# A two-layer decoder trunk on one core: down projections with 34 seven-product quads whose weight sums are made in DRAM by accumulating DMAs

## The chip, the core and the metric

The kernel runs on one core of one Trainium2 chip. A core has a matrix engine (TensorE, "PE" in the profile; its weight loads are "PEld"), a vector engine (VectorE, "DVE"), a scalar engine (ScalarE, "ACT"), GpSimd ("POOL") and SyncE ("SP"); the last two do little here but issue DMAs. Each engine runs its own instructions in order, and waits for others through semaphores. Sixteen DMA engines move the data between DRAM and the core's memory. The metric is the device time of one execution in microseconds.

## The reference

The input is 256 tokens by 2048 features in float32. Two layers follow one another, each with attention (block attention in the first, sliding window with sinks in the second) and a gated feed-forward with a causal convolution of width 3. Each half of a layer ends with a residual and a layer norm. The change lies in the feed-forward:

```python
def conv_ffn(x, w_up, conv_w, conv_b, w_down):
    h = x @ w_up                                    # 2048 -> 2 x 5504
    ...                                             # causal depthwise convolution, width 3
    g, v = jnp.split(hc, 2, axis=-1)
    return (jax.nn.gelu(g) * v) @ w_down            # 5504 -> 2048
...
h = layer_norm(ALPHA * h + ffn, ln_g[layer, 1], ln_b[layer, 1])
```

## The kernel before

All products are made in float32r from split operands: a number is held as a high part and the rest, and a product takes three matmuls (high by high, high by low, low by high). The weights come through one stream. A *half* is 128 x 1024 weights, 512 KB. `load_weights` (L98) puts the next half into one of four raw buffers by a DMA of SP's queue; `high_upto` (L113) lets ScalarE write its high part (L129), `low_piece` (L156) lets VectorE write the rest (L158). When a half is split its raw buffer is free, and the next load is issued. `take` (L202) hands the next half to TensorE and splits three halves ahead, or as far as `reach` says.

The work runs in stages: attention, output projection, up projection with convolution and gate, down projection, twice. The order on each engine is the order of the program text. A *step* is one half of weights that TensorE has used; `at(n, f)` puts the call `f` n steps further on in the program text. It sets no time by itself: an engine reaches the instruction when those before it on the same engine are done and its semaphores allow it.

In the output projection of the attention (32 halves) the dictionary `reach`, filled by `settle` (L403), makes the splits run up to 14 halves ahead of TensorE, into places of `xT`, `up` and `st` that are free then. Near its end the first 128 tokens are finished before the second 128 (`tilewise`, L345, and `late`, L583): VectorE folds in the accumulators (L435), takes the moments and norms the first tokens (L564, L565) while TensorE works on the second; TensorE then transposes the normed tokens (`turn`, L570, matmuls at L574) between its products. The last splits that `reach` asks for stand ahead of these steps on VectorE and ScalarE.

When the attention's memory is given back, `FeedForward.__call__` (L810) lets POOL load the convolution's weights `cw` (L817), and in layer 0 four copies from DRAM to DRAM, `band<-ud` (L286).

The up projection has 86 units of two halves (`ws_unit`, L296). After each unit comes a convolution on VectorE, and after each pair of units the gate and the split of the result into `st` or `up`.

The down projection (`project_out` with `paired`, and `two_chunks`, L478) works on two chunks of 512 columns at a time, 43 blocks of 128 rows each. Some blocks form *quads*: two row blocks by two column chunks, for two tiles of 128 tokens. A quad is a 2 x 2 matrix product with seven products in place of eight, on sums of the activations and sums of the weights; three sums of products go to PSUM banks of their own (`a`, `s1`, `s2`, `s3`) and are combined after the last quad. Before, there are six quads in each pair of chunks, 24 in all. VectorE makes their sums of weights from the raw halves (`quad_high`, L140, and `quad_low`, L151; the subtractions are at L137), and the sums of activations at the start of the down projection (`sums`, L443). The plain products of the other blocks lie between the quads.

```python
    for i, n in enumerate(groups):
        order += [plain.pop(0) for _ in range(n - 1)] + [(2 * i, 0)]
        quads.append(len(order) // 2)
        order += [(2 * i, 1), (2 * i + 1, 1), (2 * i + 1, 0), plain.pop(0)]
```

Of the kernel before, what the change touches and what calls it, by code (L numbers as in the profile page):

```python
# [53 lines left out]
class Quad(namedtuple("Quad", "tm uh ul bh bl")):  # L54
# [3 lines left out]
    def third(self, i):  # L58
        return self.tm[:, i * 512:(i + 1) * 512]

    def shape(self, b):
        return b.rearrange("p (a c) -> p a c", c=P)


def paired_order(lead, groups):

    plain = [(k, c) for c in range(2) for k in range(2 * PAIRS, FT)]
    order, quads = [plain.pop(0) for _ in range(lead)], []  # L70
    for i, n in enumerate(groups):
        order += [plain.pop(0) for _ in range(n - 1)] + [(2 * i, 0)]
        quads.append(len(order) // 2)
        order += [(2 * i, 1), (2 * i + 1, 1), (2 * i + 1, 0), plain.pop(0)]
    return order + plain, quads
# [3 lines left out]
def trunk(ctx: ExitStack, tc: tile.TileContext, wst, xT_in, x_in, relb, onehot, umask, sinks, conv_in, ln_g, ln_b, out):  # L79
# [11 lines left out]
    n_halves = wst.shape[0]  # L91
    raws, halves, aside, quad = {}, {}, {}, {}
# [20 lines left out]
    def high_upto(i, behind=None):  # L113
        while todo["high"] <= min(i, n_halves - 1):
# [20 lines left out]

    def minus(out, a, b):
        nc.vector.tensor_tensor(out=out, in0=a, in1=b, op=ALU.subtract)  # L137

    def quad_high(s):


        q, (wh, wl) = quad[s], placed[s]
        b11, b12, b22 = raws[s - 1][:, 512:], raws[s][:, 0:512], raws[s][:, 512:]
        t3, t1, t2 = (q.third(i) for i in range(3))
        nc.scalar.activation(q.bh, q.shape(b22), AF.Copy)
        minus(t1, b12, b11)
        minus(t3, b22, b12)
        nc.scalar.activation(wh, q.tm[:, 0:HW], AF.Copy)  # L148
        minus(t2, b22, t1)

    def quad_low(s):  # L151
        q, (wh, wl) = quad[s], placed[s]
        minus(q.bl, q.shape(raws[s][:, 512:]), q.bh.bitcast(F32))
        minus(wl, q.tm[:, 0:HW], wh.bitcast(F32))
# [5 lines left out]
    def split_upto(i, behind=None):  # L160
        while todo["low"] <= min(i, n_halves - 1):
            s = todo["low"]
            high_upto(s, behind)
            if s in quad:
                quad_low(s)
                raws.pop(s - 1)
                load_weights()
            elif len(pieces(s)) == 1:
                if s - 1 in quad:
                    q = quad[s - 1]  # L170
                    nc.scalar.activation(q.uh, q.tm[:, 512:], AF.Copy)
                low_piece(s, slice(0, HW))
                if s - 1 in quad:
                    minus(q.ul, q.tm[:, 512:], q.uh.bitcast(F32))
            placed.pop(s)
            todo["low"] += 1
            if s + 1 not in quad:
                raws.pop(s)
                load_weights()
# [86 lines left out]
    def bias_table(pool):  # L266
# [15 lines left out]
        pe_at(3, table)  # L282

# [112 lines left out]
    def project_out(src, nk, li, homes, preload, turnover=None, paired=None):  # L396
# [5 lines left out]
        w0 = nexth["i"] + (nk * NCH - WINDOW_BLOCKS) // 2  # L402
# [18 lines left out]
        gb = gbp.tile([P, 2, D], F32, name="gb")  # L421
# [24 lines left out]
        def sums(p, n):  # L446


            a, b = (xT[:, 2 * p + i:2 * (p + n):2, :] for i in range(2))
            f, sm = (gb[:, i, 0:n * 512].rearrange("p (a b) -> p a b", b=512) for i in range(2))  # L450
            x = lambda i, t: f[:, :, i * T + t * P:i * T + (t + 1) * P]
            s = lambda i: sm[:, :, (i - 1) * P:i * P]

            def whole():
                for i in range(2):
                    y = st[:, 2 * p + i:2 * (p + n):2, :].bitcast(F32)
                    nc.vector.tensor_tensor(out=f[:, :, i * T:(i + 1) * T], in0=y[:, :, 0:T], in1=y[:, :, T:2 * T],
                                            op=ALU.add)

            def combine():  # L460
                nc.vector.tensor_tensor(out=s(1), in0=x(1, 1), in1=x(0, 1), op=ALU.add)
                minus(s(2), s(1), x(0, 0))
                minus(s(3), x(0, 0), x(0, 1))
                minus(s(4), x(1, 0), s(2))

            def split():
                nc.scalar.activation(a, sm, AF.Copy)
                minus(b, sm, a.bitcast(F32))

            return whole, combine, split  # L470

        def two_chunks(n):


            order, quads = paired_order(LEAD[n // 2], GROUPS[n // 2])
            i0 = nexth["i"]
            accs = [[acc_tile(), acc_tile()], []]
            side = {}  # L478
            tail = WINDOW_BLOCKS if n else 0
            place = lambda k, t: (src(k)[:, t * P:(t + 1) * P], src(k)[:, T + t * P:T + (t + 1) * P])  # L480
            total = lambda p, i: (xT[:, 2 * p, (i - 1) * P:i * P], xT[:, 2 * p + 1, (i - 1) * P:i * P])
            begun = set()

            def product(key, acc, a, wh, wl, stop=False):
                nc.tensor.matmul(acc, a[0], wh, start=key not in begun, stop=False)  # L485
                nc.tensor.matmul(acc, a[0], wl, start=False, stop=False)  # L486
                nc.tensor.matmul(acc, a[1], wh, start=False, stop=stop)  # L487
                begun.add(key)

            def bank(name):  # L490
                if name not in side:
                    side[name] = psum.tile([P, 512], F32, name="at")
                return side[name]

            def acc(c, t):
                if not accs[c]:
                    accs[c] += [acc_tile(), acc_tile()]
                return accs[c][t]

            quads_last = lambda q: q == PAIRS - 1 and lastp[0] < 2 * quads[-1]  # L500
            lastp = {c: max(j for j, b in enumerate(order) if b[1] == c and b[0] >= 2 * PAIRS) for c in range(2)}
            halfof = lambda w, j: w[:, j * 512:(j + 1) * 512]
            for hx in range((len(order) - tail) // 2):
                i = nexth["i"]
                wh, wl = take()
                q = quads.index(hx) if hx in quads else None
                done = quads.index(hx - 1) if hx - 1 in quads else None
                if q is not None:
                    q_ = quad[i]
                    product("s1", bank("s1"), total(q, 1), halfof(wh, 1), halfof(wl, 1), stop=q == PAIRS - 1)  # L510
                    product("s3", bank("s3"), total(q, 3), halfof(wh, 0), halfof(wl, 0), stop=q == PAIRS - 1)
                    product((1, 0), acc(1, 0), total(q, 4), q_.bh, q_.bl)
                else:
                    for j in range(2):
                        k, c = order[2 * hx + j]
                        w = halfof(wh, j), halfof(wl, j)
                        if k >= 2 * PAIRS:
                            for t in range(2):
                                product((c, t), acc(c, t), place(k, t), *w, stop=2 * hx + j == lastp[c] and not (c == 0 and quads_last(PAIRS - 1)))
                        elif k % 2 == 0:  # L520
                            product("a", bank("a"), place(k, 0), *w, stop=k == 2 * PAIRS - 2)
                        else:
                            product((0, 0), acc(0, 0), place(k, 0), *w, stop=quads_last(k // 2))
                if done is not None:
                    u = quad.pop(i - 1)
                    product("s2", bank("s2"), total(done, 2), halfof(u.uh, 1), halfof(u.ul, 1), stop=done == PAIRS - 1)
                    product((0, 1), acc(0, 1), place(2 * done + 1, 1), halfof(u.uh, 0), halfof(u.ul, 0),
                            stop=quads_last(done))
# [77 lines left out]
        if paired is not None:  # L606
# [12 lines left out]
            if after:  # L619
                settle()  # L620
# [392 lines left out]
```

## Time and profile before

| | us |
|---|---|
| median of 3 runs | 2071.97 (2071.81 to 2072.13) |
| the profiled execution | 2071.78 |
| span of its profile | 2070.0 |
| TensorE busy | 2056.8 |
| VectorE busy | 1575.7 |
| ScalarE busy | 1032.4 |
| GpSimd busy | 14.6 |

| stage | from about, us |
|---|---|
| output projection, layer 0 | 300 |
| up projection, layer 0 | 388 |
| down projection, layer 0 | 871 |
| output projection, layer 1 | 1262 |
| up projection, layer 1 | 1350 |
| down projection, layer 1 | 1832 |

Times in the profile are microseconds from the start of the span. A row of a timeline has the start, the time taken, the engine, the line, the operation, the tile written and the tiles read, and in square brackets how long the engine was idle before it and what ended the wait. A row of landing times has minimum, median and maximum from the issue of a DMA to its last byte. DMA shares are means over the 16 engines.

### The profile page before, as it was taken

Reading aid. Unit: us, or ns where it says so; the run is one execution under the profiler, and the core shown is the slowest. Engines: PE = TensorE matmul, PEld = TensorE weight load, DVE = VectorE, ACT = ScalarE, POOL = GpSimd, SP = SyncE. Lnnn points to the kernel's source line nnn. Section 1 sums busy time; section 2 is a strip of 40 time slices with the busy share of each in tenths; the row PEclk is TensorE's granted clock in tenths of the full one; section 3 lists DMA queues with packets and bytes.
Section 4 is the critical chain, followed back from the end, with each engine's and each line's share of the span. In section 5 each row is a group of like instructions: output and inputs, shape, how many; then the busy total and the mean of one; then the engine's idle time right before and its main releaser. Section 6 shows DMA issues by size and latency. Waiting matters only on the chain.

```text
span 2070.0 us, 28868 instructions
## 1 busy us (share of the span) xinstructions
PE 2056.8 (99%) x11004; PEld 1777.8 (86%) x11004; DVE 1575.7 (76%) x2313; ACT 1032.4 (50%) x1456; POOL 14.6 (1%) x26
## 2 busy tenths in 40 slices
PE   9999999999999999999999999999999999999997
PEld 7888888988888888888888888898888888888886
DVE  5655556787787877898986676788787787788886
ACT  5544444455555554455553555445545454555452
POOL 0000000000000000000000000000000000000000
PEclk9999999999999999999999999999999999999999
DMA  8666558455555555576685545635555555566663
GB/s 316 215 211 206 173 166 274 142 186 192 185 190 188 192 184 193 183 243 201 204 268 185 171 148 169 236 118 197 187 191 184 192 189 188 189 216 215 193 214 132
DMA packets 116187, 405.08 MB, mean 196 GB/s; under 512 B 14112, under 2 KB 18784, under 8 KB 114768
## 3 DMA queue, kind: packets, MB, share of 16 engines
q1 hardware_dynamic: 111728, 389.96, 57.2%
q0 software_dynamic: 4032, 13.01, 1.7%
q8 instruction: 86, 1.41, 0.3%
q14 instruction: 53, 0.43, 0.1%
q10 hardware_dynamic: 288, 0.26, 0.0%
HBM read 401.02 MB, written 6.34 MB: 197 GB/s over the span
## 4 chain that ended last, share of the span: by engine, by line
PE 99%; DVE 0%; DMA 0%; ACT 0%; issue 0%
PE acc L302 38%; PE acc L305 20%; PE acc L485 6%; PE acc L486 6%; PE acc L487 6%; PE acc L355 5%; PE acc L356 5%; PE acc L357 5%; PE acc L320 1%; PE at L485 1%; PE at L486 1%; PE at L487 1%; PE acc L332 1%; PE at L655 1%; PE at L688 1%; PE at L681 1%
## 5 line engine op out<-in xcount | busy, mean ns | idle before, releaser
L158 DVE TENSOR_TENSOR wl<-raw,wh 128x1024 fp32r<-128x1024 f32 (+1 forms) x641 | 778.9, 1218 | 402.8 <-ACT wh L129 395.9
L129 ACT ACTIVATE wh<-raw 128x1024 fp32r<-128x1024 f32 (+1 forms) x641 | 675.3, 1055 | 682.0 <-PE acc L302 247.8
L302 PE MATMUL acc<-xT,wh 128*128 128x512 f32 x3456 | 872.7, 394 | 0.0
L302 PEld LDWEIGHTS acc<-xT,wh 128*128 128x128 f32 x3456 | 623.5, 189 | 112.9
L305 PEld LDWEIGHTS acc<-xT,wl 128*128 128x128 f32 x3456 | 471.4, 190 | 33.9
L305 PE MATMUL acc<-xT,wl 128*128 128x256 f32 x3456 | 481.8, 282 | 0.0
L485 PE MATMUL acc<-wh,up 128*128 128x512 f32 x360 | 140.0, 389 | 0.0
L486 PE MATMUL acc<-wl,up 128*128 128x512 f32 x360 | 140.0, 389 | 0.0
L487 PE MATMUL acc<-wh,up 128*128 128x512 f32 x360 | 140.0, 389 | 0.0
L858 DVE SCALAR_TENSOR_TENSOR work<-work,cw 128x255 f32<-128x255 f32 x172 | 83.2, 484 | 6.1
L859 DVE SCALAR_TENSOR_TENSOR work<-work,cw 128x254 f32<-128x254 f32 x172 | 83.1, 483 | 6.2
L487 PEld LDWEIGHTS acc<-wh,up 128*128 128x128 f32 x360 | 67.6, 188 | 14.1
L485 PEld LDWEIGHTS acc<-wh,up 128*128 128x128 f32 x360 | 67.6, 188 | 14.0
L486 PEld LDWEIGHTS acc<-wl,up 128*128 128x128 f32 x360 | 67.6, 188 | 13.9
L857 DVE TENSOR_SCALAR work<-work,cw 128x256 f32<-128x256 f32 x172 | 70.9, 412 | 6.2
L856 DVE TENSOR_TENSOR work<-acc,work 128x256 f32<-128x256 f32 x172 | 71.7, 417 | 1.5 <-ACT work L855 1.5
L855 ACT ACTIVATE work<-acc 128x256 f32<-128x256 f32 x172 | 63.3, 368 | 6.5 <-PE acc L332 6.5
L355 PE MATMUL acc<-wh,xT 128*128 128x512 f32 x144 | 57.5, 400 | 0.4 <-ACT xT L225 0.4
L356 PE MATMUL acc<-wl,xT 128*128 128x512 f32 x144 | 56.3, 391 | 0.0
L357 PE MATMUL acc<-wh,xT 128*128 128x512 f32 x144 | 56.3, 391 | 0.0
L196 ACT ACTIVATE work<-work 128x256 f32<-128x256 f32 x86 | 36.1, 419 | 39.2 <-DVE work L859 39.2
L148 ACT ACTIVATE wh<-work 128x1024 fp32r<-128x1024 f32 x24 | 25.5, 1063 | 47.5 <-DVE work L137 47.5
(196 smaller groups left out, 2199.8 us busy)
## 6 DMA issues: line engine op xcount, KB each, us to landing
raw<-in_wst_dram SPq DMA_DIRECT2D x721, 512.0 KB, 3.4
gb<-in_ln_g_dram POOLq DMA_DIRECT2D x4, 1024.0 KB, 6.9
gb<-in_ln_b_dram POOLq DMA_DIRECT2D x4, 1024.0 KB, 8.7
band<-ud SPq DMA_DIRECT2D x4, 512.0 KB
bias<-band SPq DMA_DIRECT2D x4, 512.0 KB, 4.3
res<-in_x_dram SPq DMA_DIRECT2D x2, 1024.0 KB, 5.5
band<-ud POOLq DMA_DIRECT2D x4, 512.0 KB, 14.2
bias<-band POOLq DMA_DIRECT2D x4, 512.0 KB, 8.3
```

Source lines behind the costliest of these rows:

```text
L129: nc.scalar.activation(wh[:, c], raws[s][:, c], AF.Copy)
L158: nc.vector.tensor_tensor(out=wl[:, c], in0=raws[s][:, c], in1=wh[:, c].bitcast(F32), op=ALU.subtract)
L302: nc.tensor.matmul(acc, cols(wh, j), xT[:, k, :], start=(k == 0), stop=False)
L305: nc.tensor.matmul(o, cols(wl, j), xT[:, k, 0:T], start=False, stop=(k == KB - 1))
L355: nc.tensor.matmul(acc, sh, wh, start=(k == 0), stop=False)
L356: nc.tensor.matmul(acc, sh, wl, start=False, stop=False)
L357: nc.tensor.matmul(acc, sl, wh, start=False, stop=(k == self.nk - 1))
L485: nc.tensor.matmul(acc, a[0], wh, start=key not in begun, stop=False)
L486: nc.tensor.matmul(acc, a[0], wl, start=False, stop=False)
L487: nc.tensor.matmul(acc, a[1], wh, start=False, stop=stop)
L858: nc.vector.scalar_tensor_tensor(c[:, 1:T], h[:, 0:T - 1], w[:, 1:2], c[:, 1:T], op0=ALU.mult, op1=ALU.add)
L859: nc.vector.scalar_tensor_tensor(c[:, 2:T], h[:, 0:T - 2], w[:, 0:1], c[:, 2:T], op0=ALU.mult, op1=ALU.add)
```

## The change

The quads become ten in the first pair of chunks of each layer, and six (layer 0) or eight (layer 1) in the second: 34 in place of 24. Their sums of weights are no longer made by VectorE. The weights of the quads are given a second time, in an input `wq`, and POOL builds the sums in DRAM tensors `t0` to `t33` by five DMAs for each quad: two plain copies of 512 KB, two accumulating ones of 512 KB and one of 256 KB. The calls are put among the steps of the up projection, eight (layer 0) or seven (layer 1) steps for a quad. A quad's sums are then two ordinary halves of the stream, loaded and split as all others, so the down projection has 58 + 52 halves in layer 0 and 58 + 55 in layer 1, where both had 86.

The sums of activations for the first eight pairs of blocks are made during the up projection, from the gated blocks, into the buffer that holds the norm's weights at other times (`gb`); they are split into `xT` at the start of the down projection. Those of the ninth and tenth pair are made during the down projection, into the same buffer, and the norm's weights are loaded after the first pair of chunks.

```diff
-PAIRS = 6
-LEAD = (16, 0)
-GROUPS = ((6, 6, 6, 6, 6, 6), (6, 4, 4, 4, 4, 4))
+QUADS = ((10, 6), (10, 8))
+LEAD = (4, 2)
+S_EARLY = 8
+QUAD_LIST = [(l, n, p) for l in range(2) for n in range(2) for p in range(QUADS[l][n])]
+def quad_halves(l, n):
+    q = QUADS[l][n]
+    plain = [(k, c) for c in range(2) for k in range(2 * q, FT)]
+    two = lambda *b: ("w", *b, *(plain.pop(0) for _ in range(2 - len(b))))
+    order = [two() for _ in range(LEAD[n])]
+    for p in range(q):
+        order += [("t", p, 0), two((2 * p, 0)), ("t", p, 1), two((2 * p + 1, 0)), two((2 * p + 1, 1))]
+    return order + [two() for _ in range(len(plain) // 2)]
...
+    tsum = {q: dram.tile([2, P, HW], F32, name=f"t{i}") for i, q in enumerate(QUAD_LIST)}
+        for n in range(2):
+            source += [tsum[l, n, h[1]][h[2]] if h[0] == "t" else wst[next(used)] for h in quad_halves(l, n)]
...
-                nc.sync.dma_start(raws[u][:, c], wst[u][:, c])
+                nc.sync.dma_start(raws[u][:, c], source[u][:, c])
...
-            if s in quad:
-                quad_high(s)
-                todo["high"] += 1
-                continue
-            if s - 1 in quad:
-                minus(quad[s - 1].third(1), raws[s][:, 0:512], quad[s - 1].third(2))
...
+    def sum_weights(q, i):
+        j, t = QUAD_LIST.index(q), tsum[q]
+        block = lambda a, b: wq[j][:, a:a + b, :]
+        half = lambda k: t[k].rearrange("p (a b) -> p a b", b=512)
+        def twice(a):
+            return bass.AP(tensor=a.tensor, offset=a.offset, ap=[a.ap[0], [0, 2], [1, 512]])
+        if i < 2:
+            nc.gpsimd.dma_start(half(i), block(i, 2))
+        if i == 2:
+            nc.gpsimd.dma_start(half(0), twice(block(3, 1)), accum_op=ALU.add)
+        if i == 3:
+            nc.gpsimd.dma_start(half(1), twice(t[0][:, 0:512]), accum_op=ALU.add)
+        if i == 4:
+            nc.gpsimd.dma_start(t[1][:, 512:], wq[j][:, 1, :], accum_op=ALU.add)
+    def plan_sums(l, n0, step):
+        for j, q in enumerate(q for q in QUAD_LIST if q[0] == l):
+            for i, m in enumerate((0, 2, 5, step + 1, step + 4)):
+                at(n0 + j * step + m, sum_weights, q, i)
...
+    def four_sums(f0, f1, out):
+        x = ((f0[:, 0:P], f1[:, 0:P]), (f0[:, P:T], f1[:, P:T]))
+        s = lambda i: out[:, (i - 1) * P:i * P]
+        minus(s(1), x[1][0], x[1][1])
+        minus(s(2), s(1), x[0][0])
+        minus(s(3), x[0][0], x[1][0])
+        nc.vector.tensor_tensor(out=s(4), in0=x[0][1], in1=s(2), op=ALU.add)
...
+            late_sums = gbp.tile([P, 2 * D], F32R, name="gb")
+            for i, p in enumerate(range(0, S_EARLY, 2)):
+                at(i + 1, split_sums, p)
+            for p in range(S_EARLY, QUADS[l][0]):
+                for i, f in enumerate(sums(p)):
+                    at(S_EARLY // 2 + 3 + 4 * (p - S_EARLY) + i, f)
...
+                    if i < 2 * S_EARLY:
+                        gs[i] = cs[0]
+                        if i % 2:
+                            at(1, sums, i // 2)
...
+            plan_sums(l, 2, (4 * FT - 20) // (sum(QUADS[l]) + 3))
```

More of the change, by code (lines that the diff above doesn't have):

```diff
@@ L47, with raw_halves, trunk @@
 OPENING = 4
-PAIRS = 6
-LEAD = (16, 0)
 TWO_ORDER = [(k, c) for k in range(12) for c in range(2)] + [(k, c) for c in range(2) for k in range(12, KB)]
-GROUPS = ((6, 6, 6, 6, 6, 6), (6, 4, 4, 4, 4, 4))
[L54 to L75, printed above, removed]
+QUADS = ((10, 6), (10, 8))
[10 more added lines that the diff above has]
+    return order + [two() for _ in range(len(plain) // 2)]
+def raw_halves(l, n):
+    return [h[1:] for h in quad_halves(l, n) if h[0] == "w"]
 @with_exitstack
-def trunk(ctx: ExitStack, tc: tile.TileContext, wst, xT_in, x_in, relb, onehot, umask, sinks, conv_in, ln_g, ln_b, out):
+def trunk(ctx: ExitStack, tc: tile.TileContext, wst, wq, xT_in, x_in, relb, onehot, umask, sinks, conv_in, ln_g, ln_b, out):
     nc = tc.nc
@@ L394, in acc_tile, with minus, project_out @@
         return psum.tile([P, 512], F32, name="acc")
-    def project_out(src, nk, li, homes, preload, turnover=None, paired=None):
+    def minus(out, a, b):
+        nc.vector.tensor_tensor(out=out, in0=a, in1=b, op=ALU.subtract)
+    def four_sums(f0, f1, out):
[5 more added lines that the diff above has]
+        nc.vector.tensor_tensor(out=s(4), in0=x[0][1], in1=s(2), op=ALU.add)
+    def project_out(src, nk, li, homes, preload, turnover=None, paired=None, early_sums=None):
         mv = Moving(src, nk)
-        w0 = nexth["i"] + (nk * NCH - WINDOW_BLOCKS) // 2
+        n_here = sum(len(quad_halves(li // 2, n)) for n in range(2)) if paired is not None else nk * NCH // 2
+        w0 = nexth["i"] + n_here - WINDOW
         n0 = w0 + WINDOW
@@ L444, in evac, with sums @@
             measure(n, t)
[L446 to L452, printed above, removed]
+        def sums(p):
+            f = paired[:, 0:2 * T].rearrange("p (a b) -> p a b", b=T)
             def whole():
                 for i in range(2):
-                    y = st[:, 2 * p + i:2 * (p + n):2, :].bitcast(F32)
-                    nc.vector.tensor_tensor(out=f[:, :, i * T:(i + 1) * T], in0=y[:, :, 0:T], in1=y[:, :, T:2 * T],
-                                            op=ALU.add)
+                    y = src(2 * p + i).bitcast(F32)
+                    nc.vector.tensor_tensor(out=f[:, i], in0=y[:, 0:T], in1=y[:, T:2 * T], op=ALU.add)
@@ L470, in sums @@
+                minus(b, paired[:, 2 * T:2 * T + 512], a.bitcast(F32))
             return whole, combine, split
[L472 to L549 removed]
```

177 lines of the change are left out of this document (105 added, 72 removed).

## The prediction

> **What bounds the kernel now.** I read the page first: the engines' busy shares, the granted clock and the chain that ended last.
>
> ```profile
> PE 2056.8 (99%) x11004; PEld 1777.8 (86%) x11004; DVE 1575.7 (76%) x2313; ACT 1032.4 (50%) x1456; POOL 14.6 (1%) x26
> ...
> PEclk9999999999999999999999999999999999999999
> ...
> PE 99%; DVE 0%; DMA 0%; ACT 0%; issue 0%
> ```
>
> TensorE works without a gap at full clock, and the chain is its own matmuls. So an instruction taken from it shortens the run by its whole duration, work taken from another engine gains nothing, and every wait that reaches TensorE is paid in full. The next question is what one product costs. The timeline of TensorE in the down projection, first and last of 28 matmuls in a row:
>
> ```profile
> 899.81 0.39 PE L486 MATMUL at<-wl,st 128*128 128x512 f32 x1
> ...
> 905.93 0.39 PE L486 MATMUL acc<-wl,up 128*128 128x512 f32 x1
> ```
>
> They overlap, so the price is the distance of their starts: (905.93 - 899.81) / 27 = 0.227 us, not the 0.39 of the row.
>
> With no slack on TensorE, the load of weights matters next. Every 512 KB half is loaded, then split by ScalarE (L129) and VectorE (L158). The stretches of the ScalarE split (length; busy us; number of splits; clock; DMA share; GB/s):
>
> ```profile
> 335.00:372.00 37.00, 21.87 (x21) 1.00 0.84 275
> 1280.00:1331.00 51.00, 29.28 (x28) 1.00 0.79 269
> 321.00:336.00 15.00, 4.65 (x5) 1.00 0.91 311
> 348.00:370.00 22.00, 12.74 (x12) 1.00 0.85 282
> 450.00:850.00 400.00, 151.67 (x143) 1.00 0.58 189
> ```
>
> The last row is the up projection: 400/143 = 2.80 us per half, DMA engines 58% busy, easy. The first two are the attention's output projections, where `reach` splits 14 halves ahead of TensorE, so that the layer norm finds VectorE free. There the ring of four raw buffers runs as fast as it can: 37/21 = 1.76, 51/28 = 1.82, 22/12 = 1.83 us per half; call it 1.8. The row of 321 to 336 belongs to the same phase, but takes 15/5 = 3.0 us per half. What differs is POOL's queue:
>
> ```profile
> 313.49 0.54 POOL L817 DMA_DIRECT2D cw<-in_conv_dram  x1 [290.10 <-ACT wh L129]
> 314.06 4.36 POOL L286 DMA_DIRECT2D band<-ud  x4
> ...
> 1275.02 0.54 POOL L817 DMA_DIRECT2D cw<-in_conv_dram  x1 [150.86 <-ACT wh L129]
> ```
>
> Four copies from DRAM to DRAM, 2 MB, run beside the loads. The queues' rows for 318 to 335 us (packets, MB, share of 16 engines):
>
> ```profile
> q1 hardware_dynamic: 866, 3.14, 53.4%
> q0 software_dynamic: 1936, 2.06, 38.5%
> ```
>
> And the landing times of the loads, issued at 318 to 330 us and at 335 to 372:
>
> ```profile
> DMA to landing us min/median/max: 7.6/8.0/8.2
> ...
> DMA to landing us min/median/max: 3.3/4.4/5.4
> ```
>
> So a copy of POOL's takes from the loads: the wait for a half nearly doubles, and the split stream slows from 1.8 to 3.0 us. Before, that lasted some 15 us and reached nobody.
>
> **The change part by part.** *Products.* Each quad replaces eight products of three matmuls by seven. Ten more quads: 30 matmuls fewer, 30 x 0.227 = -6.8 us. That is the whole gain.
>
> *VectorE and ScalarE in the down projection.* The sums of weights (L137) and their special splits leave, 51 plain splits come (223 halves instead of 172). All of it stands under a TensorE that doesn't wait: 0. In the up projection 64 small VectorE operations (128x128) are added:
>
> ```profile
> 450.00:850.00 400.00, 400.00 (x2292) 351.97 (x2291) 318.67 (x500) 201.43 (x287) 0.00 (x0) 1.00 0.58 189
> 377.31 0.26 DVE L553 BATCH_NORM_AGGREGATE ag<-stats 128x2 f32<-128x24 f32 x1
> ...
> L856 DVE TENSOR_TENSOR work<-acc,work 128x256 f32<-128x256 f32 x172 | 71.7, 417 | 1.5 <-ACT work L855 1.5
> ```
>
> Between 0.26 and 0.42 us each they are 17 to 27 us, in a stretch where VectorE is busy 319 of 400 us; taken as hidden, 0; without that cover, those 17 to 27.
>
> *The sums by DMA.* Five copies for each quad, 512 + 512 KB plain and 512 + 512 + 256 KB accumulating: 2.36 MB; 16 quads in layer 0 (37.7 MB), 18 in layer 1 (42.5 MB). `plan_sums` spreads them over the steps of the up projection, but a step only orders instructions within one engine. POOL does nothing else there, and the sums wait for nothing but earlier DMAs of POOL. In its queue they stand right behind `cw` and the bands. So I expect them to start at 318 us and at 1275 us, in the output projections, 50 to 70 us ahead of the up projection: just where the loads have no room.
>
> What this costs: in layer 0 the copies follow the bands, so 21 halves (335 to 372) go on at up to 3.0 instead of 1.8 us: 21 x 1.2 = 25 us late. In layer 1, 28 x 1.2 = 34 us. Who notices: in program order the first half of the norm stands behind these splits on VectorE, and TensorE's transposes wait for the norm. The timelines of VectorE and TensorE (two layers):
>
> ```profile
> 373.61 2.34 DVE L158 TENSOR_TENSOR up<-raw,up 128x1024 fp32r<-128x1024 f32 x2
> 375.87 0.68 DVE L435 SCALAR_TENSOR_TENSOR res<-res,acc 128x512 f32<-128x512 f32 x1
> ...
> 378.82 0.75 DVE L565 SCALAR_TENSOR_TENSOR res<-res,rs,gb 128x512 f32<-128x512 f32 x1
> ...
> 380.81 0.60 PE L574 MATMUL at<-ident,res 128*128 128x128 f32 x4
> ...
> 1337.09 0.69 DVE L435 SCALAR_TENSOR_TENSOR res<-res,acc 128x512 f32<-128x512 f32 x1 [3.61 <-PE acc L357]
> ...
> 1340.04 0.75 DVE L565 SCALAR_TENSOR_TENSOR res<-res,rs,gb 128x512 f32<-128x512 f32 x1
> ...
> 1342.34 0.60 PE L574 MATMUL at<-ident,res 128*128 128x128 f32 x4
> ```
>
> Layer 0: VectorE comes from the last split without a pause, and the norm's first piece ends at 379.57, 1.2 us before its transposes: slack 1.2 us. Layer 1: 3.6 us idle and 1342.34 - 1340.79 = 1.6: slack 5.2 us. What is late beyond that stops TensorE.
>
> How much of the time do the sums fill their queue? The bounds: never in the way, 0 us; always, as the bands, 25.2 - 1.2 + 33.6 - 5.2 = 52 us. At the bands' pace (2.06 MB in 17 us, 0.121 MB/us) a quad's copies take 19.5 us. Two of its accumulations wait for the copy before them. A small transfer of this queue shows the fixed part:
>
> ```profile
> cw<-in_conv_dram POOLq DMA_DIRECT2D x2, 172.0 KB, 3.2
> ```
>
> 172 KB at that pace are 1.5 us, so about 1.7 us are fixed, with 1.1 us to issue (4.36 / 4 of the bands); two such pauses of 3 us make 19.5 / 25.5 = 0.76, if nothing of another quad fills them. Against that, the accumulations move rows of 2 KB, the loads rows of 4 KB, so their turns may be shorter, at worst half: 0.4. I take 0.6, nearer the bands: 0.6 x 25.2 - 1.2 = 13.9 and 0.6 x 33.6 - 5.2 = 15.0, together +28.9 us.
>
> The Trainium skill (Collectives: The Full Stack, The bandwidth ceiling: the fold count and why AG ≠ RS ≠ AR) says that an add in the DMA path reads two sources, and so moves at half the rate. No run here shows it yet. By it a quad costs as much as 3.67 MB, and the sum would go by the upper bound, 52 us, instead of 28.9.
>
> *Up projection under the sums.* At full presence the loads manage 3.0 us per half, 2.80 are needed; at 0.6, 1.8 + 0.6 x 1.2 = 2.5, enough: 0 (a rival below).
>
> *Loads of the down projection.* Five halves per quad in 39 matmuls: 39 x 0.227 / 5 = 1.77 us per half, as fast as the ring was ever seen (1.76 to 1.83). Short by at most 0.06 x 5 = 0.3 us per quad; three halves split ahead give 3 x 1.77 less a split of 2.3 = 3 us. I take 1 us for both layers; 0 to 10 (34 x 0.3, no lead). A load of a sum waits for its last accumulation, with all loads behind it in SP's queue; but 16 x 25.5 us after 318 is 726, the down projection starts at 871: 0.
>
> Sum on the profiled execution: -6.8 + 28.9 + 1 = +23.1. Its span is 2070.0, its time 2071.8 (1.8 around it), 0.2 under the median of the runs; so 2071.8 + 23.1 = 2095.
>
> **The rivals.**
> 1. *The sums stay out of the way* (faster). If accumulating copies are slow in waiting but light on the DMA engines, below a presence of some 0.05 in layer 0 and 0.15 in layer 1 (slack over full lateness), only the products count: 2065.2. For it: the engines are 16% free in the prefetch. Against it: the loads use that room already, and the bands did slow them. Up to 2.6 us of stalls it stays faster by over 0.2%.
> 2. *A draw.* Presence of about 0.25, stalls of 25.2 x 0.25 - 1.2 + 33.6 x 0.25 - 5.2 = 8, or the down projection's ring short by its full 10 with nothing else: 2068 to 2076.
> 3. *The sums starve the up projection too.* Full presence: +52, and 3.0 - 2.8 = 0.2 us per half while they last. Layer 0: 37.7 / 0.121 = 312 us from 318 on, of which 225 after the opening, 80 halves, 16 us; layer 1: 351 us from 1275, 263 after its opening, 94 halves, 19 us; less 3 us of lead each: 2071.8 - 6.8 + 52 + 29 + 1 = 2147. For it: VectorE has 64 operations more there. Against it: waits in the sums' own chain. By the rule of the Trainium skill above (Collectives: The Full Stack, same section) the sums last 1.55 times as long, which makes this case worse by some 26 us, an estimate from that page.
>
> **How the numbers follow.** Likeliest, 0.50: stalls in the output projections, 2095; its own range is 2077 to 2125 (a presence of 0.3, and of 1 with 7 us more in the down projection). Sums out of the way 0.23; draw 0.10; starving 0.17. The range 2064.5 to 2125 holds the first three. Faster or slower counts beyond 0.2% (4.1 us), about what a measurement of this kernel can tell: faster 0.23, same 0.10, slower 0.50 + 0.17 = 0.67.
>
> **What would show it.** Right: POOL's sums start near 318 and 1275 us; the median landing of loads between 335 and 372 us rises from 4.4 to 6 us or more; TensorE stands idle ahead of the transposes of the first normed tokens, some 14 us in each layer, released by VectorE; 30 matmuls fewer. Wrong: sums that start with the up projection, landings unchanged, or TensorE idle in the down projection for want of loads rather than at the norms. If TensorE shows no gap at all, the time is 2065.

## The result, and the profile after

| | before | after |
|---|---|---|
| median, us | 2071.89 | 2104.66 (2101.43 to 2107.77, 4 runs) |
| ratio, with 95% interval | 1 | 1.0158 (1.0140 to 1.0176) |
| the profiled execution, us | 2071.78 | 2101.43 |
| span of its profile, us | 2070.0 | 2099.7 |

The changed kernel is slower, by 32.8 us at the median; its profiled execution, the fastest of the four, by 29.7. From the page of the kernel after (engines, granted clock in fortieths of the span, the DMA queues with packets, MB and share, the chain that ended last):

```profile
PE 2058.1 (98%) x10974; PEld 1776.7 (85%) x10974; DVE 1547.2 (74%) x2292; ACT 1049.0 (50%) x1467; POOL 151.4 (7%) x196
...
PEclk9999999899999999999999999989999999999999
...
q0 software_dynamic: 37216, 93.24, 20.0%
...
PE 89%; DMA 7%; DVE 2%; ACT 1%; issue 0%; ACTq 0%; POOL 0%; DVEq 0%; POOLq 0%
```

30 matmuls are gone (10974 for 11004). But the chain no longer consists of TensorE alone: DMA has 7% of it, and in two of the forty slices, around 390 and 1390 us, the granted clock is below full. The timeline of POOL gives the start of the sums (L260 a plain copy, L262 the first accumulating one), in both layers:

```profile
313.59 0.55 POOL L829 DMA_DIRECT2D cw<-in_conv_dram  x1 [290.38 <-ACT wh L124]
314.16 4.30 POOL L276 DMA_DIRECT2D band<-ud  x4
318.45 1.09 POOL L260 DMA_DIRECT2D t<-in_wq_dram  x2
335.61 1.10 POOL L262 DMA_DIRECT2D t<-in_wq_dram  x1 [16.07 <-DMA t<-in_wq_dram]
...
1291.14 0.54 POOL L829 DMA_DIRECT2D cw<-in_conv_dram  x1 [150.87 <-ACT wh L124]
1291.68 1.05 POOL L260 DMA_DIRECT2D t<-in_wq_dram  x2
```

They stand right behind the bands, and in layer 1 right behind `cw` (16 us later than before, since the whole layer is). Both are in an output projection, 88 and 91 us ahead of the up projection whose steps were to carry them (it starts at 406.8 and 1382.7 us). The loads beside them, by the stretches of ScalarE's split (L124 here; length, busy us, number of splits, clock, DMA share, GB/s) and by the landing times of loads issued between 335 and 372 us:

```profile
335.00:372.00 37.00, 15.19 (x15) 1.00 1.01 303
...
1296.00:1347.00 51.00, 21.12 (x20) 1.00 1.03 306
...
450.00:850.00 400.00, 152.65 (x145) 1.00 0.82 251
```

```profile
DMA to landing us min/median/max: 7.6/8.4/9.1
```

15 splits where 21 were, 20 where 28 were (the stretch of layer 1 moved by its 16 us): 2.47 and 2.55 us per half for 1.76 and 1.82. The median landing went from 4.4 to 8.4 us. The third row is the up projection, with 145 halves in 400 us where 143 were: nothing is late there. In the output projection the DMA engines are full, and the two queues share their time evenly, though not the bytes (packets, MB, share, from 335 to 372 us):

```profile
q0 software_dynamic: 1568, 3.82, 49.6%
...
q1 hardware_dynamic: 2022, 7.35, 50.8%
```

The share is the time that the packets took, so it does not tell whether the engines themselves or the DRAM behind them set the limit. Who pays is seen on VectorE, at the end of the output projection of layer 0:

```profile
390.40 1.22 DVE L133 TENSOR_TENSOR up<-raw,up 128x1024 fp32r<-128x1024 f32 x1 [3.16 <-ACT up L124]
391.93 1.23 DVE L133 TENSOR_TENSOR up<-raw,up 128x1024 fp32r<-128x1024 f32 x1 [0.30 <-ACT up L124]
393.07 0.68 DVE L438 SCALAR_TENSOR_TENSOR res<-res,acc 128x512 f32<-128x512 f32 x1
...
396.02 0.75 DVE L577 SCALAR_TENSOR_TENSOR res<-res,rs,gb 128x512 f32<-128x512 f32 x1
```

and on TensorE, which ran out of products and waited for the norm:

```profile
382.48 0.39 PE L347 MATMUL acc<-xT,st 128*128 128x512 f32 x1
396.82 1.11 PE L586 MATMUL at<-ident,res 128*128 128x128 f32 x4 [13.96 <-DVE res L577]
...
398.17 0.63 PE L346 MATMUL acc<-up,st 128*128 128x512 f32 x1
398.59 0.63 PE L347 MATMUL acc<-up,st 128*128 128x512 f32 x1
...
1372.46 1.11 PE L586 MATMUL at<-ident,res 128*128 128x128 f32 x4 [11.95 <-DVE res L577]
```

The wait for loads has become a wait for VectorE: the splits (L133) come late, the fold and the norm (L438, L577) stand behind them, the transposes (L586) behind those. Two idle times of 13.96 and 11.95 us follow. The matmuls after them start 0.42 us apart (398.17 to 398.59) instead of 0.227, which the granted clock explains (busy time and count of the five engines, then the clock and the DMA engines; both layers):

```profile
382.00:398.00 16.00, 2.04 (x9) 1.55 (x8) 11.65 (x16) 4.95 (x6) 1.69 (x3) 0.60 1.01 295
398.00:400.00 2.00, 2.00 (x6) 1.52 (x6) 1.97 (x4) 0.60 (x1) 2.00 (x3) 0.50 0.80 259
...
402.00:406.00 4.00, 4.00 (x22) 3.34 (x21) 1.38 (x2) 2.02 (x4) 0.00 (x0) 0.95 1.05 182
...
1361.00:1374.00 13.00, 1.53 (x6) 1.44 (x7) 11.90 (x17) 5.67 (x8) 1.58 (x2) 0.65 1.03 296
...
1378.00:1382.00 4.00, 4.00 (x22) 3.24 (x21) 1.10 (x2) 2.06 (x4) 0.95 (x2) 0.93 0.08 28
```

A mean of 0.60 over 16 us at either 1 or 0.5 is 3.2 us at full clock, so it fell at about 385.2, some 2.4 us after the last matmul ended (382.87); 0.95 over 4 us is 0.4 us more at half, so it rose at about 402.4, 5.6 us after work resumed at 396.8. Those 5.6 us at half clock did the work of 2.8. In layer 1 the same working gives a fall at about 1364.9, 4.4 us after the last matmul ended (1360.5), and a rise at about 1378.6, 6.1 us after work resumed: 3.1 us lost.

The bill, by TensorE's timelines: the end of the output projection of layer 0 moved from 388.1 to 406.8 us, by 18.7, and that of layer 1 took 17.1 longer: 35.8 us. Less 6.8 for the products is 29.0; 29.7 was measured on the spans. The up and down projections have no new gap of 0.5 us in this execution. The median lies another 3.2 us above it, which no profile covers.

### The profile page after: what moved, and what is told of

The parts are those of the page before. It is cut to its first block, busy times and chain, and to the rows that moved or that the text cites. A ratio compares the mean times of both kernels' runs of the same rounds, so it can differ in the third digit from the quotient of the medians.

```text
span 2099.7 us, 29222 instructions
## 1 busy us (share of the span) xinstructions
PE 2058.1 (98%) x10974; PEld 1776.7 (85%) x10974; DVE 1547.2 (74%) x2292; ACT 1049.0 (50%) x1467; POOL 151.4 (7%) x196
## 3 DMA queue, kind: packets, MB, share of 16 engines
q0 software_dynamic: 37216, 93.24, 20.0%
## 4 chain that ended last, share of the span: by engine, by line
PE 89%; DMA 7%; DVE 2%; ACT 1%; issue 0%; ACTq 0%; POOL 0%; DVEq 0%; POOLq 0%
PE acc L292 38%; PE acc L295 20%; DMA raw<-in_wst_dram 6%; PE acc L546 4%; PE acc L545 4%; PE acc L547 4%; PE acc L345 3%; PE acc L347 3%; PE acc L346 3%; PE acc L310 1%; PE at L546 1%; PE at L547 1%; PE at L545 1%; DMA raw<-t 1%; DVE wl L133 1%; PE acc L322 1%
## 5 line engine op out<-in xcount | busy, mean ns | idle before, releaser
L133 DVE TENSOR_TENSOR wl<-raw,wh 128x1024 fp32r<-128x1024 f32 (+1 forms) x716 | 870.7, 1218 | 447.0 <-ACT wh L124 438.6
L124 ACT ACTIVATE wh<-raw 128x1024 fp32r<-128x1024 f32 (+1 forms) x716 | 755.4, 1056 | 709.1 <-DMA raw<-in_wst_dram 218.3
L545 PE MATMUL acc<-wh,up 128*128 128x512 f32 x336 | 130.8, 389 | 0.0
L546 PE MATMUL acc<-wl,up 128*128 128x512 f32 x336 | 130.8, 389 | 0.0
L547 PE MATMUL acc<-wh,up 128*128 128x512 f32 x336 | 130.7, 389 | 0.0
L260 POOL DMA_DIRECT2D t<-in_wq_dram x68 | 76.1, 1119 | 0.0
L547 PEld LDWEIGHTS acc<-wh,up 128*128 128x128 f32 x336 | 63.1, 188 | 13.2
L545 PEld LDWEIGHTS acc<-wh,up 128*128 128x128 f32 x336 | 63.1, 188 | 13.1
L546 PEld LDWEIGHTS acc<-wl,up 128*128 128x128 f32 x336 | 63.1, 188 | 13.0
L264 POOL DMA_DIRECT2D t<-t x34 | 35.6, 1046 | 345.1 <-issue 174.7
L133 DVE TENSOR_TENSOR up<-raw,up 128x1024 fp32r<-128x1024 f32 x30 | 36.5, 1221 | 29.6 <-ACT up L124 29.5
L345 PE MATMUL acc<-wh,xT 128*128 128x512 f32 x144 | 57.8, 401 | 0.0
```

What stands on the lines that cost most here:

```text
L124: nc.scalar.activation(wh[:, c], raws[s][:, c], AF.Copy)
L133: nc.vector.tensor_tensor(out=wl[:, c], in0=raws[s][:, c], in1=wh[:, c].bitcast(F32), op=ALU.subtract)
L260: nc.gpsimd.dma_start(half(i), block(i, 2))
L345: nc.tensor.matmul(acc, sh, wh, start=(k == 0), stop=False)
L545: nc.tensor.matmul(bank(key), a[0], wh[:, c], start=key not in begun, stop=False)
L546: nc.tensor.matmul(bank(key), a[0], wl[:, c], start=False, stop=False)
```

## The experiments

All times are medians in us. Each kernel stands against the kernel before run on the same chip, 2071.9 to 2072.2. The expectations name runs by the marks in brackets.

| kernel | sums | quads | time | ratio, 95% interval |
|---|---|---|---|---|
| after | early | 34 | 2104.66 | 1.0140 to 1.0176 |
| 1 late sums (e1) | with the up projection | 34 | 2071.29 | 0.9989 to 1.0006 |
| 2 plain copies (e3) | early, no add | 34 | 2109.24 | 1.0170 to 1.0198 |
| 3 before plus sums (e5) | early, unread | 24 | 2111.64 | 1.0161 to 1.0200 |
| 4 no sums, from `wq` (e4) | none | 34 | 2083.32 | 1.0039 to 1.0067 |
| 5 no sums, from the stream (e7) | none | 34 | 2069.62 | 0.9979 to 0.9997 |
| 6 late sums, late `gb` (e6) | with the up projection | 34 | 2076.83 | 1.0015 to 1.0035 |
| 7 no sums, late `gb` (e9) | none | 34 | 2078.13 | 1.0016 to 1.0034 |
| 8 28 quads, late `gb` (e8) | with the up projection | 28 | 2073.12 | 0.9994 to 1.0011 |
| 9 28 quads, early `gb` (e10) | with the up projection | 28 | 2073.33 | 0.9998 to 1.0016 |
| 10 28 quads, held `gb` (e11) | with the up projection | 28 | 2070.09 | 0.9982 to 0.9999 |
| 11 30 quads, held `gb` (e12) | with the up projection | 30 | 2069.33 | 0.9978 to 0.9997 |
| 12 34 quads, held `gb` (e13) | with the up projection | 34 | 2069.14 | 0.9977 to 0.9995 |

### 1. The sums held until the up projection

A small VectorE operation of the up projection's step, and a POOL copy that reads it, hold POOL's queue. Nothing else changes.

```diff
+    def hold_sums(l, j):
+        g = stat.tile([P, 2], F32, name=f"hold{l}_{j}", bufs=1)
+        nc.vector.memset(g[:, 0:1], 0.0)
+        nc.gpsimd.tensor_copy(out=g[:, 1:2], in_=g[:, 0:1])
...
+        at(n0, hold_sums, l, 0)
```

> The changed kernel, with one edit: a one-column VectorE write at the first step of each up projection, and a one-column GpSimd copy that waits for it, ahead of the first sum of each layer. Theory 'room' (the sums cost time only because they take DMA turns from the weights' loads during the two output projections): sums start near 407 and 1368 us instead of 318 and 1292, no stall of TensorE at the transposes, 2071.9 - 6.8 + 1 = 2066 (2065 to 2069). Rival 'anywhere' (the sums starve the loads wherever they run): the stalls move into the up projection, 2085 or more.

Measured: 2071.29 (2068.81 to 2076.11, 11 runs), no change against before, and 33.4 us faster than after. The stretch of the splits, then the landing of loads issued from 968 to 980 us, while POOL's 2 MB of norm weights (`gb`, issued at 969.9) move, and the timeline of TensorE behind them:

```profile
335.00:372.00 37.00, 22.01 (x22) 1.00 0.85 285
```

```profile
DMA to landing us min/median/max: 4.4/8.4/10.7
```

```profile
992.62 0.50 PE L552 MATMUL at<-wl,xT 128*128 128x512 f32 x1 [1.41 <-DVE wl L133]
```

With the sums away the output projection is as before (22 halves in 37 us), and the up projection bears the same sums with gaps of TensorE of 0.6 us in all. So their place was the cost, not their amount. But the 6.8 us of the products do not appear: TensorE's gaps (starts over 0.26 us apart, what they are beyond 0.227, from 10 us on) are 16.6 us in all, 11.3 before, the new ones mostly in the down projections. The largest group there, 2 us at 989 to 993, follows the load of `gb`, beside which a half took 8.4 us (4.5 for those issued from 905 to 968).

### 2. The same copies without the add

The three accumulating copies of each quad become plain ones of the same bytes and waits; the sums of weights are then not formed.

```diff
-            nc.gpsimd.dma_start(half(0), twice(block(3, 1)), accum_op=ALU.add)
+            nc.gpsimd.dma_start(half(0), twice(block(3, 1)))
...
```

> The changed kernel with the three accumulating copies of each quad made plain copies of the same bytes, so the weights' sums are wrong. Theory 'room': POOL's queue is still full during the output projections, its packets only take less of the engines (a plain quad 5.9 us of each engine by the rows of 84 ns for 2 KB and 159 ns for 4 KB, an accumulating one 9.6 us by 176 ns for 2 KB), so a good part of the stalls stays: 2080 to 2098. Rival 'adding' (the read-modify-write of DRAM is what hurts the loads): stalls all but gone, 2065 to 2072.

Measured: 2109.24 (2108.09 to 2114.01), not faster than after. The queue of the sums over the whole span, from its page:

```profile
q0 software_dynamic: 26336, 93.24, 14.7%
```

The accumulating copies are dear to the DMA engines: the same 93.24 MB are 14.7% here and 20.0% with it. Less the 35 us (1.7% of 2070.0) that this queue's other transfers took before, the sums' copies are 385 us of 16 engines with the add and 275 without. By bytes 35.7 of their 80.2 MB are plain in both, 122 us; so the rest cost 263 against 153, 1.7 times, if a plain byte costs the same in both runs. Taken packet by packet, the accumulating copies are 21760 packets of 2 KB and 286 us, and the plain ones in their place 10880 of 4 KB and some 151 us (at the mean of that queue's 4 KB packets): 1.9 times. The smaller packets come with the add, so the two are not told apart. And yet the stall stays: 14.18 us of idle time ahead of the transposes of layer 0, for 13.96. Lighter copies run through sooner and take the place more densely (4.66 MB for 3.82 between 335 and 372 us, 14 splits for 15). Both expectations wanted a shorter time from lighter copies, and both were wrong: the stall needs no adding, and it does not shrink with the weight of the copies.

### 3. The kernel before, with the sums beside it

The kernel before, to which the 170 copies are added at the same steps; nobody reads what they make.

```diff
+            plan_sums(l, 2, (4 * FT - 20) // (sum(QUADS[l]) + 3))
```

> The kernel before, with the changed kernel's 170 copies added on POOL at the same places; nobody reads what they make. Theory 'room': the stalls of the changed kernel alone, without its gain: 18.7 + 17.1 us more, 2071.9 + 36 = 2108 (2100 to 2114). Rival 'order' (the stall needs the changed order of splits or the loads of sums): 2072 to 2076.

Measured: 2111.64 (2101.52 to 2113.08, 4 runs), 39.5 us above the kernel before. The change cost 32.8 after saving 6.8 of products, so its sums cost 39.6: the same, within the spread of these runs. The splits between 335 and 372 us, and TensorE's wait for the norm (us in total, times, longest):

```profile
335.00:372.00 37.00, 13.79 (x13) 1.00 0.98 289
```

```profile
PE at L604 <- DVE res L595: 25.9, 2, 14.0
```

In the kernel after the same wait reads 25.9, 2, 14.0 too. No other part of the change (quads, sums of activations, order of the down projection) is needed for the loss.

### 4 and 5. No sums at all

In both, POOL makes no sums. In 4 the two halves of a quad's sums are read from `wq` (the first of the two added lines), in 5 from halves of the ordinary stream (the second); the products of the quads are then formed with other weights than their sums.

```diff
-            source += [tsum[l, n, h[1]][h[2]] if h[0] == "t" else wst[next(used)] for h in quad_halves(l, n)]
+            source += [wq[QUAD_LIST.index((l, n, h[1]))][:, 2 * h[2]:2 * h[2] + 2, :].rearrange("p a b -> p (a b)") if h[0] == "t" else wst[next(used)] for h in quad_halves(l, n)]
+            source += [wst[2 * h[1] + h[2]] if h[0] == "t" else wst[next(used)] for h in quad_halves(l, n)]
...
-            plan_sums(l, 2, (4 * FT - 20) // (sum(QUADS[l]) + 3))
```

> The changed kernel without the sums: the halves that hold sums are loaded straight from the input of quad weights, two blocks each, and POOL makes no copies, so the output leaves the sums out. Theory 'room': only the 30 products fewer and the 51 more halves of the down projections are left, 2065 to 2067. Rival 'down' (the denser loads of the down projection cost a part): 2069 to 2076 with idle TensorE inside the down projections.

Measured: 2083.32, slower than both theories had it, with some 14 us of small gaps over the down projections. From its page, the loads of the sums' halves (KB each, median us to landing):

```profile
raw<-in_wq_dram SPq DMA_DIRECT2D x68, 512.0 KB, 5.1
```

They land in 5.1 us, while those from `t` landed in 4.5 in the kernel after. `wq` holds the four blocks of a quad side by side, so a half has rows of 4 KB, one every 8 KB; a half of `t` or of the stream is contiguous.

> The changed kernel without the sums, the halves of sums loaded from whole halves of the weight stream (contiguous 512 KB) instead of two blocks out of four of the quad weights (rows of 4 KB at a pitch of 8 KB), so the output leaves the sums out. If the slow run without sums came from that source's layout: landing median back from 5.3 to 4.5 us, 2067 to 2072. Rival (the denser loads alone cost it): 2080 or more again.

Measured: 2069.62 (2067.41 to 2074.06). So 13.7 us of 4's loss was its source, by its place or its layout (not told apart). 5 is the change without any sum: 2.6 us faster than before, not 6.8. The gaps that are left stand in the dense stretches: 0.61 us at 991, 2.63 from 1944.6 to 1953.5, 1.24 from 1990 to 1999. The first two follow POOL's loads of `gb` (issued at 969.4 and 1929.7 us; the halves issued from 1926 to 1940 landed in 8.6 us). So of the some 4 us that are missing, most again goes with `gb`, and 1.24 at most is the quads' loads by themselves.

### 6, 7 and 8. The norm's weights later

`gb` was loaded beside the quads' loads of the second pair of chunks. Here it is held behind the last quad of that pair; 7 has no sums (as 5, with the same substitution of weights); 8 has eight quads in the first pair and six in the second, and one more half of plain products after each quad of the first pair.

```diff
-            at(1, load_gb)
+            late_gb = LEAD[1] + 5 * QUADS[l][1] + 1
+            at(late_gb, hold_sums, l, 1)
+            at(late_gb, load_gb)
```

> The kernel with late sums, and the load of the norm's weights (gb, 2 MB on POOL's queue) held back in the same way until the second pair of chunks has done its quads (33 steps into it in layer 0, 43 in layer 1). Theory 'down' (the loads of the down projection run at their limit, so that 2 MB beside them in the dense part stop TensorE): the idle time near 970 to 993 us goes, 2067 to 2070 where the kernel with late sums had 2071.3; layer 1 gains less, since its last halves are dense as well. Rival 'noise' (those stalls have nothing to do with gb): 2071.3 again.

Measured: 2076.83, worse than 1. Loads issued from 1045 to 1056 us, beside `gb` at 1047, and the wait that it ends in:

```profile
DMA to landing us min/median/max: 4.4/9.7/10.1
```

```profile
1094.62 0.89 PE L592 MATMUL at<-ident,res 128*128 128x128 f32 x4 [4.69 <-DVE res L583]
```

The fault of the change in small: 2 MB of POOL's have moved into the next prefetch ahead of a norm, loads take 9.7 us there, and TensorE waits for the norm 45 us later, with the clock below full behind it (0.50 from 1095 to 1098 us).

> The changed kernel without the sums (source as whole halves of the weight stream; the output leaves the sums out) and with late gb. Theory 'room' and 'down' together: nothing of POOL's beside the dense loads, 2065 to 2067, the gain of 30 products in full. If it stays at 2069 or more, the denser loads cost by themselves.

Measured: 2078.13. Without any sums the same late load costs 8.5 us against 5 (2069.62), so this loss is `gb`'s alone. It does not speak for the expectation's last sentence: nearly all of its new gaps stand behind `gb`, at 1090 to 1104 and 2044 to 2047 us, and none of 0.5 us in the quads' dense stretches.

> The kernel with late sums and late gb, with eight and six quads per pair of chunks (28 in all) and one more half of plain blocks after each quad of the first pair, so that six halves come in 51 matmuls (1.93 us each) instead of five in 39 (1.77). Theory 'down': no stalls left, 12 matmuls fewer than before: 2071.9 - 2.7 + 0.5 = 2069.7, with less spread between runs than with 34 quads. Rival: loads are not the limit there, then 28 quads are worse than 34 by six products, some 4 us.

Measured: 2073.12. The small gaps of the dense stretches are gone, the wait at the norm is not (2.54 us of idle time at 1092.8).

### 9. 28 quads, `gb` where the change has it

As 8, without the hold on `gb`.

> The sums start with the up projection (as in e1), 28 quads in place of 34 (eight in the first pair of chunks, six in the second), one more block of plain products between the quads of the first pair, and the norm's weights loaded where the changed kernel loads them, not just ahead of the next norm. The theory (full loads ahead of a norm cost the stall, a stream of halves that needs 1.77 us each in the quads costs the small gaps of the down projection): four quads more than before are 12 matmuls fewer, 12 x 0.227 = 2.7 us; no stall above 1 us at any norm, gaps of TensorE in all no more than 0.5 us above those of before, so 2069 to 2070. The rival (the sums cost something of their own wherever they stand, by the chip's DRAM or DMA engines): no better than the kernel of the same form with the late load, 2073, and gaps in the down projection.

Measured: 2073.33, as the rival had it, but not by the rival's reason. With no sum of the first pair left in its buffer, POOL issues `gb` at 886.3, as soon as that is free, 84 us sooner than in 1, beside the first quads of the down projection. Landing of loads issued from 885 to 892 us, and ScalarE's wait:

```profile
DMA to landing us min/median/max: 3.1/9.3/9.8
```

```profile
897.13 2.10 ACT L126 ACTIVATE wh<-raw 128x1024 fp32r<-128x1024 f32 x2 [6.78 <-DMA raw<-t]
```

TensorE lost 2.1 us at 898 to 900 and 1.0 at 1860 to 1862, and nothing at the norm. So this run moved the collision once more, and did not tell the two theories apart.

### 10, 11 and 12. `gb` where the stream has room

The load is held until the last quad of the first pair, where plain products follow, which TensorE uses at 2.7 us per half. 10 has 8 and 6 quads in each layer, without 8's extra halves; 11 has 8 and 6, then 8 and 8; 12 has the changed kernel's 34, and four instead of two halves ahead of the second pair's quads.

```diff
+            at(LEAD[0] + 5 * QUADS[l][0], make_gb)
+            at(LEAD[0] + 5 * QUADS[l][0], hold_sums, l, 1)
+            at(LEAD[0] + 5 * QUADS[l][0], load_gb)
             accs = two_chunks(0)
...
-            at(1, load_gb)
```

> The sums start with the up projection, 28 quads, no extra plain products between them, and POOL's load of the norm's weights (2 MB) held until the last quad of the first pair of chunks, where eleven halves of plain products are left, which TensorE uses at 6 x 2 x 0.227 = 2.7 us a half while the ring can bring one every 1.8. The theory (any 2 MB of POOL's that meet the stream where it has no room cost 2 to 14 us, and nothing where it has room): 11 x (2.7 - 1.8) = 10 us of room for a load worth some 7 us, so no gap above 0.5 us after it and none at the norm: the 12 matmuls fewer count, 2072.1 - 2.7 + 0.5 = 2070, faster than before. The rival (the sums or the quads' dense loads cost by themselves): 2072 or more, as in the kernels with 28 quads so far, gaps inside the quads' stretch of the down projection.

Measured: 2070.09 (2069.23 to 2070.77). From its page and the landing of loads issued from 956 to 968 us, beside `gb` at 957.9:

```profile
PE 2054.0 (99%) x10992; PEld 1776.5 (86%) x10992; DVE 1531.8 (74%) x2259; ACT 1030.5 (50%) x1454; POOL 127.7 (6%) x170
...
PE 99%; DVE 0%; DMA 0%; ACT 0%; issue 0%
```

```profile
DMA to landing us min/median/max: 3.7/4.5/6.2
```

The chain is TensorE's again, and TensorE's gaps are 11.3 us in all, as before. Of the 2.7 us of 12 matmuls, 1.9 show at the median.

> As the kernel before in this list, with eight quads instead of six in the second pair of chunks of layer 1: 30 quads, 18 matmuls fewer than before. The theory: 18 x 0.227 = 4.1 us less, 2072.1 - 4.1 + 1 = 2069, as the second pair has no load of POOL's in it. The rival (dense loads cost by themselves): 2072 or more, with gaps inside the quads' stretches.

Measured: 2069.33 (2068.57 to 2070.58), as the theory had it.

> All 34 quads of the changed kernel, the sums held until the up projection, POOL's load of the norm's weights held until the last quad of the first pair of chunks, and four halves of plain products instead of two ahead of the quads of the second pair. After the load's start 4 + 4 halves of plain products pass, 8 x (2.7 - 1.8) = 7 us of room for a load worth some 7 us, with three halves split ahead besides. The theory: all 30 products saved count, less what the quads' dense stretches of ten lose (0 to 3 us): 2071.9 - 6.8 + 0 to 3 = 2065 to 2068. The rival (dense loads cost by themselves, more with each quad): 2069 or more, not better than the kernel with 30 quads, gaps inside the quads' stretches.

Measured: 2069.14 (2066.04 to 2072.58), 1 us above the theory's range, and no better than 11, as the rival said. The gaps are not in the quads' stretches, though. All that is new, 2.8 us, stands behind them, in the last plain products of layer 1 (2033 to 2043 us), here by VectorE's timeline and then TensorE's:

```profile
2033.71 0.69 DVE L444 SCALAR_TENSOR_TENSOR res<-res,work 128x512 f32<-128x512 f32 x1
2034.32 1.22 DVE L133 TENSOR_TENSOR xT<-raw,xT 128x1024 fp32r<-128x1024 f32 x1
2035.46 1.28 DVE L449 BATCH_NORM_STATS2 stats<-res 128x6 f32<-128x512 f32 x2
```

```profile
2035.59 0.50 PE L352 MATMUL acc<-xT,up 128*128 128x512 f32 x1 [0.81 <-DVE xT L133]
```

With eight quads in the last pair their banks are combined close to the end, and VectorE, without a pause there, is late with its splits. 11 has the same quads there, and 1.8 us of gaps. Of the kernels that form the sums, 10, 11 and 12 are the ones that beat both before and after, and before by only 0.1%. The wider spread of 12 says that other executions lose elsewhere; where is open.

## Why the prediction was right, and where it was short

- *Where the sums start.* Right: 318.45 us as said, and in layer 1 right behind `cw`. Runs 1 and 3 show that their place is the cause.
- *What they do to the loads.* Right in kind and in size: 2.5 us per half was forecast, 2.47 and 2.55 were measured. The landing median rose to 8.4 us, where 6 or more was named. That the presence of 0.6 fits so well is in part luck. It was chosen between 0.76 and 0.4 for the pauses of the queue and for its shorter rows, and no run tests these reasons; run 2, with larger packets, has 37/14 = 2.64 us per half, which is 0.7.
- *The stall ahead of the transposes.* Right: 13.96 and 11.95 us, released by VectorE, for 13.9 and 15.0.
- *The sum of the stalls, +28.9, is the term that was too small.* The output projections lost 35.8. The idle time alone came to 29.5, close to the forecast: 13.96 and 11.95 us, and 1.7 and 1.8 in short waits for late splits before them. The 15.0 for layer 1 was 3 us too long, and the short waits made up for it. What the sum left out is the half clock after each stall, 2.8 and 3.1 us. The Trainium skill (TensorE: Matmul & The Clock Gate, Part 1: The HAM clock gate (the "warmup" mystery)) has the rule that was left unused: after an idle window of about 3.4 us the clock is halved, and it comes back after some 3.4 us of sustained work. The trace agrees in kind, not in size: its clock fell some 2.4 and 4.4 us after the last matmul and rose 5.6 and 6.1 after the first.
- *Products, -6.8.* Right here to 0.7 us (35.8 less the 29.7 measured is 6.1), but it is not what the change could have brought: without any sums (run 5) 2.6 us remain, with late sums (run 1) 0.9. The term for *the loads of the down projection*, 1 us of 0 to 10, was about 4 in run 5. It weighed the quads' loads alone, and did not count the 2 MB of `gb` that meet them; with `gb` held (run 12) no gap is left in the quads' stretches. In the profiled execution of the kernel after, none showed either.
- *Up projection under the sums, 0.* Right, and it stays right with all sums in it (run 1). The third rival falls.
- *The weight of the add.* The upper bound of 52 us by the rule of the Trainium skill (Collectives: The Full Stack, The bandwidth ceiling: the fold count and why AG ≠ RS ≠ AR) was not reached, though the half rate, which the Trainium skill states there for collectives, is not far from the 1.7 to 1.9 times of run 2. The weight decides how long the sums last (layer 0: from 318 to 674 us with the add, to 604 without), not how much of the prefetch they take.
- *The median* of 2104.66 is within the range; 2095 was 10 us short, 6.9 by the output projections and most of the rest by the 3.2 us that only other executions have.

## What to carry to other kernels

A step in program text does not delay a DMA whose queue has nothing else to wait for: it starts as soon as its engine gets there, so give it a true dependency on the place where it may run. Bulk copies cost what the tightest load stream beside them loses, here nearly twice the landing time, and that is paid tens of microseconds later at the next point where an engine's order puts a norm behind the splits. When a transfer is moved, look for what it meets in its new place: `gb` cost something in three places and nothing in the fourth.

## What the runs showed of the hardware

- TensorE, idle for 12 to 14 us, came back at half clock for 5.6 and 6.1 us, so each of these stalls cost some 3 us more than it lasted. After 4.7 us of idle time (run 6) the clock was below full as well; after 2.54 us (run 8) it stayed at full.
- Accumulating copies from DRAM to DRAM, in packets of 2 KB, took 1.7 to 1.9 times as much of the DMA engines as plain ones of the same bytes, mostly in packets of 4 KB (run 2).
- Beside POOL's copies, SP's loads had half of the busy DMA engines' time (50.8% and 49.6%), and landed in 8.4 us where 4.4 was the median before.
- Halves of 4 KB rows at 8 KB distance landed in 5.1 us, where contiguous ones from another tensor took 4.5 (run 4 and the kernel after). The kernel with the slower halves took 13.7 us more than run 5; layout and place in DRAM were not told apart.
